# Odd mixer of a decoder step: the pool branch's square-product weights are made one round ahead, in tiles of the attention's pool

## The chip, the cores and the metric

The kernel runs on one core of one Trainium2 chip. The metric is the device time of one execution in microseconds (us), from the first to the last instruction of the program and what lies around it. Less is better.

## The reference, cut to what matters

The reference is one inference step of a two-layer decoder trunk for 512 prompt rows and 32 sample rows (544 in all, width 1024). Each layer is half a SwiGLU block, a mixer, and another half SwiGLU block. The change lies in the mixer of layer 1, the odd mixer:

```python
def odd_mixer(xn, w_in, w_out, c_lin_w, c_scale, ...):
    proj = xn @ w_in                                   # 1024 -> 1024 (pool) + 1536 (q, k, v)
    yc, new_pool = mixer_c(proj[..., :C_WIDTH], pool_state, start_pos, c_lin_w, c_scale)
    q, k, v = d_qkv(proj[..., C_WIDTH:], q_norm, k_norm)
    yd = sliding-window attention of q, k, v (16 heads, window 128, sinks, bias)
    y = jnp.concatenate([yc, yd], axis=-1) @ w_out

def mixer_c(...):                                      # four groups of 256 columns, windows 2, 4, 8, 16
    for gi, win in enumerate(C_WINDOWS):
        pooled = (sum over the last win rows) / count - cur[..., sl]
        outs.append(jnp.einsum('blc,cd->bld', pooled, lin_w[gi]))     # square product, 256 x 256
    y = jnp.concatenate(outs, axis=-1) * scale
```

The two branches, pool (C) and attention (D), need nothing of each other. They meet only in the product with `w_out`.

## The kernel before, in words

Activations lie with the 1024 columns on partitions, eight tiles of 128 by 544. A product in f32 precision is made of three products of halves: each operand is split into a high and a low part (`h`, `l` of an activation; `wh`, `wl`, or `w` for both, of a weight), and `mm` (L208) issues, for each of its k-tiles, high by high, high by low and low by high, in two halves of 272 columns. An accumulator `acc` of `mm` is written by 48 matmuls when the product has eight k-tiles, by 12 when it has two.

`unit` (L185 on) loads up to eight k-tiles of a weight by 256 columns into a staging tile `S` (the pool `stg`, two buffers, DMA issued on SP), and its inner function `part(j)` makes the two halves of 128 columns: ScalarE writes the high part (L193), VectorE the low part (L194). Without `alloc` the halves lie in the pool `wp`, two buffers each; with `alloc` both halves lie in one tile of the pool that `alloc` names. `RR` takes a tile of the pool `rot` (six buffers in the odd mixer), `AA` a tile of the pool `aux` (14 buffers in the odd mixer). `aux` serves the attention: the scores `sc` (two tiles a block), the transposed weights `pT`, the value tiles `vt`, and some fifteen tiles of the sample attention.

`odd` is written in this order: keys and values; four groups `kv` of four heads, each with its query product, query norms (16 small products, L1440, and a chain of twelve small VectorE operations) and four blocks of 128 rows; then the pool branch; then the product with `w_out` for the pool half (`out_proj(w_out, 0, ...)`), and for the attention half.

- A block of the attention is `att_probs` (scores on TensorE, L1514; bias and scale L1518, row maximum L1520 to L1527 on VectorE; four exponentials and one more, L1531 and L1533, on ScalarE; sum, reciprocal and weights, L1534 to L1539, on VectorE) and, one block later in the program, `att_out` (transposes L1553, copies L1555, products with the values L1558, copies L1561). Block 0 of a group is half as wide as the others. `sample_attention` (L1615 on) is made in five steps, interleaved with the last group.
- The pool branch has five rounds, `i` from 0 to 4. In round `i` below 4, `pooled(3 - i)` makes the input product of group `3 - i` (two accumulators of 48 matmuls, weights in `wp`), takes it out of PSUM as `pc` (L1575, L1577), and after the `yield` makes the window sums on GpSimd (`ta`, `tb`, L1599) and the pooled rows `pl` (L1602 on). In round `i` above 0, the square product of group `4 - i` is made: `c_lin_w` is loaded by `unit` with `alloc=RR`, and two accumulators of 12 matmuls follow.

What an engine does is set by the order of its own queue. The program text is not that order: a scheduler takes the instructions in the order of the text as a priority, gives out the buffers of each pool, runs a timeline of its own, and writes one fixed list of instructions for each engine. So instructions of the pool branch can be put between those of the attention, although they stand behind it in the text, wherever their operands and buffers are there in that timeline. An instruction that waits at the head of its engine's list holds back all that stands behind it on that engine.

Of the kernel before, what the change touches and what calls it, by code (L numbers as in the profile page):

```python
# [93 lines left out]
class Trunk:  # L94
# [26 lines left out]
    def TT(self, s, dt=F32):  # L121
        return self.big.tile([P, T], dt, name=self.nm(s), tag="T")
# [29 lines left out]
    @staticmethod  # L152
    def two(ap):
        return ap.rearrange("p (a b) -> p a b", a=2)
# [1174 lines left out]
    def odd(self, nxt):  # L1329
        nc, I, O, two, bc, ch, C = self.nc, self.I, self.O, self.two, self.bc, self.ch, self.C  # L1330
# [3 lines left out]
        sm, RR, TT, AA, ps_ = self.small, self.RR, self.TT, self.AA, self.ps  # L1334
# [35 lines left out]
        for c0, lst, alloc in ((2048, kn, TT), (2304, vf, RR)):  # L1370
            un = self.unit(w_in, 0, 8, c0)
            for j in range(2):
                acc = self.mm(un(j), 8, xs)
# [51 lines left out]
        for kv in range(4):  # L1425
            un = self.unit(w_in, 0, 8, 1024 + kv * 256)
            q2 = []
            for j in range(2):
                acc = self.mm(un(j), 8, xs)
# [35 lines left out]
        yc, pool = [], []  # L1465
        npp = sm("npp", [P, 8, 15])
        nps = sm("nps", [P, 8, 32])

        for i in range(5):
            if i < 4:  # L1470
                stage = self.pooled(3 - i, ext, npp, nps, pool)
                next(stage)
            if i:
                un = self.unit(I["c_lin_w"][0, 4 - i], 0, 2, 0, alloc=RR)
                for j in range(2):
                    m = (4 - i) * 2 + j
                    acc = self.mm(un(j), 2, pool[i - 1])
                    y = TT("yc")
                    with self.tc.high_priority():
                        S.activation(two(y), acc[:, :, :HT], AF.Copy, scale=csc[:, m:m + 1])  # L1480
                    yc.append(y)
            if i < 4:
                next(stage, None)
# [252 lines left out]
    def later(self, odd):  # L1736

        yield from self.columns_gen(("b_norm_g", "c_scale", "a_ln_g", "a_ln_b"), self.TT, self.nc.gpsimd)
        if odd:
            yield from self.bias_pattern()  # L1740
# [80 lines left out]
```

## Time and profile before

| | us |
|---|---|
| median of 3 runs (lowest to highest) | 2270.87 (2264.91 to 2271.98) |
| the profiled execution's own time | 2267.51 |
| its span, first to last instruction | 2265.7 |
| TensorE busy (share of the span) | 2238.1 (99%) |
| VectorE busy | 1708.2 (75%) |
| ScalarE busy | 1063.1 (47%) |
| GpSimd busy | 587.4 (26%) |

The mean granted TensorE clock is 0.994 of full speed. Times in the text are us from the start of the span. In the trace's rows PE is TensorE, PEld its weight load, DVE VectorE, ACT ScalarE, POOL GpSimd, and SPq the DMA queue of SyncE. A row of the timeline has the start, the length, the engine, the line, the operation, what is written and read, the shape, the count of merged instructions, and in brackets the engine's idle time ahead of it with what ended it. Matmuls overlap each other, so their pace is read from start to start.

### The profile page before, as it was taken

What the parts mean: (1) busy time and instruction counts of PE and PEld (TensorE: products, weight loads), DVE (VectorE), ACT (ScalarE), POOL (GpSimd) and SP (SyncE); (2) the same over time, 40 slices, a digit from 0 to 9 for tenths busy, and PEclk for the clock granted to TensorE, in tenths of its full rate; (3) what the DMA queues carried; (4) which work ended last, traced back from release to release, by engine and by line L of the source; (5) the groups of instructions that cost most, each with busy time, mean ns of one, the idle gap of its engine ahead of it and who ended that gap; (6) DMA issues with size and microseconds to landing.
All of it is one profiled execution on the core that took longest, in us unless ns stands there. A gap on an engine that the chain in (4) does not pass through costs nothing.

```text
span 2265.7 us, 42894 instructions
## 1 busy us (share of the span) xinstructions
PE 2238.1 (99%) x17456; PEld 2177.3 (96%) x17456; DVE 1708.2 (75%) x2837; ACT 1063.1 (47%) x1937; POOL 587.4 (26%) x500
## 2 busy tenths in 40 slices
PE   8999999999999999999999999999999999999999
PEld 7999999998889999999999999999988899999998
DVE  7978887675468779888777887876578757888874
ACT  6444444543346354444454444443356544444442
POOL 0434340023330014332403333322033002333320
PEclk9999999999999999999999999999999999999999
DMA  4344443322433233323232332334313223323322
GB/s 149 95 115 99 122 101 114 111 78 76 130 102 96 98 90 103 110 84 110 84 108 63 110 92 89 105 108 142 107 57 114 80 79 107 91 89 106 92 87 68
DMA packets 313862, 224.29 MB, mean 99 GB/s; under 512 B 11640, under 2 KB 306960, under 8 KB 313664
## 3 DMA queue, kind: packets, MB, share of 16 engines
q1 hardware_dynamic: 307800, 206.15, 29.9%
q0 software_dynamic: 5680, 15.34, 2.8%
q8 instruction: 137, 2.24, 0.4%
q14 instruction: 61, 0.50, 0.1%
q10 hardware_dynamic: 184, 0.06, 0.0%
HBM read 203.76 MB, written 17.75 MB: 98 GB/s over the span
## 4 chain that ended last, share of the span: by engine, by line
PE 90%; DVE 4%; ACT 2%; DMA 2%; issue 1%; POOL 1%; SPq 0%; POOLq 0%; DVEq 0%; ACTq 0%
PE acc L208 45%; PE ps L254 34%; PE acc L654 2%; DMA S<-in_ffn_w_gu_dram 1%; PE acc L687 1%; PE ps L974 1%; PE ps L1514 1%; PE ps L1558 1%; POOL S L227 1%; PE ps L1553 1%; DVE wl L237 0%; PE ps L966 0%; POOL S L226 0%; PE ps L368 0%; DVE wl L245 0%
## 5 line engine op out<-in xcount | busy, mean ns | idle before, releaser
L254 PE MATMUL ps<-h,wh 128*128 128x272 f32 x2100 | 602.6, 289 | 5.8 <-ACT g L525 5.8
L254 PE MATMUL ps<-l,wh 128*128 128x272 f32 x2100 | 604.8, 289 | 0.0
L254 PE MATMUL ps<-h,wl 128*128 128x272 f32 x2100 | 602.1, 288 | 0.0
L208 PE MATMUL acc<-h,wh 128*128 128x272 f32 x2768 | 588.7, 292 | 2.0 <-DVE x L694 1.0
L208 PE MATMUL acc<-l,wh 128*128 128x272 f32 x2768 | 585.7, 291 | 0.2 <-DVE l L264 0.2
L208 PE MATMUL acc<-h,wl 128*128 128x272 f32 x2768 | 584.5, 291 | 0.0
L208 PEld LDWEIGHTS acc<-h,wh 128*128 128x128 f32 x2768 | 437.6, 189 | 11.1 <-issue 6.2
L208 PEld LDWEIGHTS acc<-l,wh 128*128 128x128 f32 x2768 | 437.6, 189 | 9.6 <-issue 8.7
L208 PEld LDWEIGHTS acc<-h,wl 128*128 128x128 f32 x2768 | 437.0, 189 | 7.8 <-issue 6.8
L254 PEld LDWEIGHTS ps<-h,wh 128*128 128x128 f32 x2100 | 395.7, 189 | 6.7 <-ACT g L525 6.7
L254 PEld LDWEIGHTS ps<-l,wh 128*128 128x128 f32 x2100 | 396.6, 189 | 0.0
L254 PEld LDWEIGHTS ps<-h,wl 128*128 128x128 f32 x2100 | 396.0, 189 | 0.0
L244 ACT ACTIVATE wh<-S 128x512 fp32r<-128x512 f32 x375 | 235.1, 629 | 322.1 <-PE ps L254 131.7
L245 DVE TENSOR_TENSOR wl<-S,wh 128x512 fp32r<-128x512 f32 x375 | 293.3, 788 | 40.9 <-ACT wh L244 37.9
L228 POOL TENSOR_TENSOR S<-S 128x512 f32<-128x512 f32 x75 | 116.9, 1558 | 509.3 <-DMA S<-in_ffn_w_gu_dram 392.6
L226 POOL TENSOR_TENSOR S<-S 128x512 f32<-128x512 f32 x75 | 102.8, 1371 | 513.3 <-DMA S<-in_ffn_w_gu_dram 235.9
L244 ACT ACTIVATE wh<-D 128x384 fp32r<-128x384 f32 (+1 forms) x224 | 120.7, 540 | 240.9 <-PE ps L254 177.2
L694 DVE SCALAR_TENSOR_TENSOR x<-acc,x 128x544 f32<-128x544 f32 x224 | 160.7, 719 | 65.1 <-PE acc L208 55.4
L245 DVE TENSOR_TENSOR wl<-D,wh 128x384 fp32r<-128x384 f32 (+1 forms) x224 | 176.5, 788 | 9.2 <-ACT wh L244 3.8
L237 DVE TENSOR_TENSOR wl<-S,wh 128x1024 fp32r<-128x1024 f32 x101 | 157.7, 1561 | 12.8 <-ACT wh L236 10.9
L193 ACT ACTIVATE wh<-S 128x1024 fp32r<-128x1024 f32 (+1 forms) x89 | 93.4, 1050 | 156.6 <-PE acc L208 129.8
L236 ACT ACTIVATE wh<-S 128x1024 fp32r<-128x1024 f32 x101 | 106.9, 1059 | 80.8 <-PE ps L254 48.7
(477 smaller groups left out, 2950.6 us busy)
## 6 DMA issues: line engine op xcount, KB each, us to landing
S<-in_ffn_w_gu_dram SPq DMA_DIRECT2D x176, 512.0 KB
D<-in_ffn_w_down_dram SPq DMA_DIRECT2D x96, 384.0 KB
S<-in_ev_w_in_dram SPq DMA_DIRECT2D x18, 1024.0 KB
S<-in_od_w_in_dram SPq DMA_DIRECT2D x10, 1024.0 KB
D<-in_ffn_w_down_dram SPq DMA_DIRECT2D x16, 512.0 KB
S<-in_ev_w_out_dram SPq DMA_DIRECT2D x8, 1024.0 KB
S<-in_od_w_out_dram SPq DMA_DIRECT2D x8, 1024.0 KB
xd<-x POOLq DMA_DIRECT2D x16, 272.0 KB, 2.5
```

Source lines behind the costliest of these rows:

```text
L193: nc.scalar.activation(hi[:, :nk, :n], src, AF.Copy)
L208: self.nc.tensor.matmul(acc[a][:, :HT] if type(acc) is list else acc[:, a, :HT], w[:, k, :], r[:, a * HT:(a + 1) * HT], start=k == order[0 ...
L226: G.tensor_tensor(t["S1"], u0, u1, op=ALU.add)
L227: G.tensor_tensor(t["S2"], t["S1"], g0, op=ALU.subtract)
L228: G.tensor_tensor(t["S3"], g0, u0, op=ALU.subtract)
L236: self.nc.scalar.activation(hi, src, AF.Copy)
L237: self.nc.vector.tensor_tensor(lo, src, hi.bitcast(F32), op=ALU.subtract)
L244: self.nc.scalar.activation(hi, src, AF.Copy)
L245: self.nc.vector.tensor_tensor(lo, src, hi.bitcast(F32), op=ALU.subtract)
L254: self.nc.tensor.matmul(acc, a[:, j, :], r, start=start and j == 0 and q == 0, stop=stop and j == 3 and q == 2, skip_group_check=True)
L654: self.nc.tensor.matmul(acc[a][:, :HT], w[:, k, :], r[:, a * HT:(a + 1) * HT], start=k == 0 and i == 0, stop=k == 7 and i == 2)
L694: nc.vector.scalar_tensor_tensor(two(self.x[m]), acc[:, :, :HT], 0.5, two(self.x[m]), op0=ALU.mult, op1=ALU.add)
```

## The change

In the loop of five rounds, the weights of the square product are now asked for at the head of the round ahead of the one that uses them: in round `i` below 4, ahead of `pooled(3 - i)`, the kernel loads `c_lin_w` of group `3 - i` and makes both halves, `cl = [un(0), un(1)]`. Round `i` above 0 uses the pair that round `i - 1` made. The pair lies in tiles of `aux` (`alloc=AA`), where it lay in tiles of `rot` (`alloc=RR`). The number of loads, of weight halves and of matmuls is the same.

```diff
+        cl = None
         for i in range(5):
+            ws = cl
             if i < 4:
+
+                un = self.unit(I["c_lin_w"][0, 3 - i], 0, 2, 0, alloc=AA)
+                cl = [un(0), un(1)]
                 stage = self.pooled(3 - i, ext, npp, nps, pool)
                 next(stage)
             if i:
-                un = self.unit(I["c_lin_w"][0, 4 - i], 0, 2, 0, alloc=RR)
                 for j in range(2):
                     m = (4 - i) * 2 + j
-                    acc = self.mm(un(j), 2, pool[i - 1])
+                    acc = self.mm(ws[j], 2, pool[i - 1])
```

Lines behind the change move down by four: L1514 of before is L1518 now, L1553 is L1557, L1558 is L1562.

TensorE, second group of heads, from the middle of block 1's `att_out` to block 3's scores. Before, with the pool branch's product of group 2 (`acc_20818`) around the attention's transposes, value products and scores:

```order
L208 MATMUL acc_20818<-l_18584,wh_20814 128x272 x2
L208 MATMUL acc_20818<-h_18583,wl_20815 128x272 x2
L208 MATMUL acc_20818<-h_18618,wh_20814 128x272
L1558 MATMUL ps_19657<-pT_19663,vt_19021 64x256 x2
L1553 MATMUL ps_19667<-cst,sc_19585 128x128 x2
L1553 MATMUL ps_19667<-cst,sc_19592 128x128 x2
L1514 MATMUL ps_19679<-ks_18991,q_19437 128x256
L1514 MATMUL ps_19679<-ks_18991,q_19492 128x256
L1514 MATMUL ps_19686<-kv_18805,q_19437 128x256
L1514 MATMUL ps_19686<-kv_18805,q_19492 128x256
L208 MATMUL acc_20818<-h_18618,wh_20814 128x272
L208 MATMUL acc_20818<-l_18619,wh_20814 128x272 x2
```

The same place now; `acc_20723` is the second accumulator of group 3's product, and these are its last matmuls:

```order
L208 MATMUL acc_20723<-h_18653,wl_20720 128x272 x2
L1557 MATMUL ps_19658<-cst,sc_19585 128x128 x2
L1557 MATMUL ps_19658<-cst,sc_19592 128x128 x2
L1562 MATMUL ps_19657<-pT_19663,vt_19021 64x256 x2
L1557 MATMUL ps_19667<-cst,sc_19585 128x128 x2
L1557 MATMUL ps_19667<-cst,sc_19592 128x128 x2
L1518 MATMUL ps_19679<-ks_18991,q_19437 128x256
L1518 MATMUL ps_19679<-ks_18991,q_19492 128x256
L1518 MATMUL ps_19686<-kv_18805,q_19437 128x256
L1518 MATMUL ps_19686<-kv_18805,q_19492 128x256
L1562 MATMUL ps_19657<-pT_19672,vt_19021 64x256 x2
L1557 MATMUL ps_19710<-cst,sc_19628 128x128 x2
```

From here to the last product of the sample attention (L1729 now) TensorE's list holds no L208 at all; it goes on with group 2 (`acc_20834`) right behind it. In the list of before, 735 matmuls of L208 stand between the same two places: the input products of groups 2, 1 and 0, the four square products and about half of `out_proj` for the pool half.

ScalarE, where the first pair of square-product weights is made. Before, in the second of the four groups of heads, between the exponentials of its blocks 2 and 3:

```order
L1533 ACTIVATE es_19644<-es_19644 128x4
L1555 ACTIVATE pT_19672<-ps_19667 128x512
L193 ACTIVATE wh_21010<-S_21006 128x1024
L193 ACTIVATE w_20934<-S_20932 128x256
L1561 ACTIVATE q_19437<-ps_19657 128x128
```

Now, behind the copies of the last block's transposes (`pT_20599`) and the first copy of the sample attention's output (`sos_20605`):

```order
L1559 ACTIVATE pT_20590<-ps_20585 128x512
L1559 ACTIVATE pT_20599<-ps_20594 128x512
L1726 ACTIVATE sos_20605<-ps_20606 128x256
L193 ACTIVATE w_20650<-S_20648 128x256
L193 ACTIVATE w_20653<-S_20648 128x256
L193 ACTIVATE w_20820<-S_20818 128x256
L193 ACTIVATE w_20823<-S_20818 128x256
L1565 ACTIVATE q_20133<-ps_20584 128x128
L1565 ACTIVATE q_20188<-ps_20584 128x128
L1726 ACTIVATE sos_20605<-ps_20617 128x256
L193 ACTIVATE wh_20830<-S_20826 128x1024
```

The first pair, and the second with it, is made at the end of the attention, and the input weights of group 2 (`wh_20830`) are made behind them.

SP's list, where `S_20648`, `S_20656`, `S_20818` and `S_20826` take the two staging buffers in turn; now:

```order
L171 DMA S_20648<-in_c_lin_w_dram 128x2x256
L171 DMA S_20656<-in_od_w_in_dram 128x8x256
L171 DMA S_20818<-in_c_lin_w_dram 128x2x256
L1667 DMA out_new_k_win_sample_dram<-kc_20333 124x2x256
L1667 DMA out_new_k_win_sample_dram<-kc_20343 124x2x256
L1667 DMA out_new_k_win_sample_dram<-kc_20412 124x2x256
L1667 DMA out_new_k_win_sample_dram<-kc_20422 124x2x256
L171 DMA S_20826<-in_od_w_in_dram 128x8x256
```

Before, the input weights of groups 3 and 2 (`S_20648` and `S_20810` there) were loaded ahead of the first `c_lin_w`; now the load of group 2's input weights (`S_20826`) stands behind the two loads of `c_lin_w` and waits for the staging buffer of the first of them.

## The prediction

> **What bounds the kernel now.** The page first: which engine is full.
>
> ```profile
> span 2265.7 us, 42894 instructions
> PE 2238.1 (99%) x17456; PEld 2177.3 (96%) x17456; DVE 1708.2 (75%) x2837; ACT 1063.1 (47%) x1937; POOL 587.4 (26%) x500
> ```
>
> TensorE is busy in 99% of the span: the kernel is as long as its list of matmuls, and an edit elsewhere gains only where TensorE waits. So the next views are TensorE's waits from 1560 to 1800, around the pool branch, and busy time by stretches there (length, then PE, PEld, DVE, ACT, POOL, granted clock, DMA).
>
> ```profile
> PE acc L208 <- ACT w L193: 1.1, 1, 1.1
> PE acc L208 <- ACT h L263: 0.9, 2, 0.6
> ```
>
> ```profile
> 1690.00:1700.00 10.00, 8.07 (x58) 6.91 (x55) 8.78 (x31) 5.14 (x18) 4.73 (x7) 1.00 0.31 80
> ```
>
> ```profile
> 1679.00:1830.00 151.00, 148.13 (x1103) 129.11 (x1102) 111.19 (x331) 82.72 (x227) 32.41 (x37) 0.97 0.28 92
> ```
>
> ```profile
> 1679.00:1830.00 151.00, 106.77 (x739) 98.31 (x738) 0.97 0.28 92
> ```
>
> The largest wait is the one that the change speaks to: the square product waits 1.1 us for its weights, and 1690 to 1700 has 1.93 us without a matmul. But from 1679 to 1830, where pool branch, attention and half of the first output product run, TensorE stands idle for only 151.0 - 148.1 = 2.9 us. That is all that earlier weights can give back: 0.13%, under the 0.3% (6.8 us) that a measurement of this kernel can tell from no change. The last row is the same stretch with L208 alone: 739 matmuls. They fill TensorE while the attention's chain of small steps runs.
>
> **What the change takes away.** The lists of the changed program, shown above, carry the prediction. With the weight pair in the attention's pool, its tile comes free, in the scheduler's timeline, only when the attention is over. The first pair is made on ScalarE behind the copy of the sample attention's first output, and group 2's input weights stand behind it. TensorE's list has from the middle of the second group of heads to the end of the attention no L208 at all. The work itself is unchanged: as many matmuls, loads and casts as before; but 735 matmuls move from beside the attention to behind it. So the sum has two terms: how long the attention takes by itself (X, from 1679), and the moved matmuls behind it.
>
> The moved matmuls, at their pace in an undisturbed place, and the attention's steps on TensorE:
>
> ```profile
> 1688.44 0.41 PE L208 MATMUL acc<-h,wl 128*128 128x272 f32 x2
> 1688.69 0.41 PE L208 MATMUL acc<-h,wh 128*128 128x272 f32 x2
> ```
>
> ```profile
> 1684.21 0.65 PE L1558 MATMUL ps<-pT,vt 128*64 128x256 f32 x4
> 1684.79 0.66 PE L1553 MATMUL ps<-cst,sc 128*128 128x128 f32 x4
> 1685.38 0.48 PE L1514 MATMUL ps<-ks,q 64*128 64x256 f32 x1
> ...
> 1686.45 0.39 PE L208 MATMUL acc<-h,wh 128*128 128x272 f32 x1
> ```
>
> Two L208 start every 0.25 us, so 739 take 92.4 us. Before, attention and fill together took 151.0; now they take X + 92.4. **The change is X - 58.6 us.** At X = 58.6 nothing is lost. A full block costs TensorE 2 x 0.58 for value products, 2 x 0.59 for transposes and 1.07 for scores, 3.4 us; what matters is how long its chain takes. One block of the second group ran nearly undisturbed:
>
> ```profile
> 1673.46 1.65 DVE L1518 SCALAR_TENSOR_TENSOR sc<-ps,rq,bias 128x256 f32<-128x256 f32 x4
> 1675.03 1.26 DVE L1520 TENSOR_REDUCE mx<-sc 128x2 f32<-128x512 f32 x2
> ...
> 1676.73 0.16 DVE L1527 TENSOR_TENSOR es<-mx,sink 128x4 f32<-128x4 f32 x1
> ...
> 1678.93 0.17 DVE L1534 TENSOR_TENSOR den<-den,es 128x4 f32<-128x4 f32 x1 [1.02 <-ACT es L1533]
> 1679.13 0.18 DVE L1535 RECIPROCAL den<-den 128x4 f32<-128x4 f32 x1
> 1679.35 1.14 DVE L1539 TENSOR_SCALAR sc<-sc,den 128x256 f32<-128x256 f32 x4
> ```
>
> ```profile
> 1676.73 0.51 ACT L1531 ACTIVATE sc<-sc,mx 128x256 f32<-128x256 f32 x1 [2.24 <-DVE mx L1524]
> ...
> 1678.71 0.19 ACT L1533 ACTIVATE es<-es 128x4 f32<-128x4 f32 x1
> ```
>
> VectorE: bias, maximum and three short ones from 1673.46 to 1676.89; then it needs ScalarE's five exponentials, 1676.73 to 1678.90; sum, reciprocal and weights end at 1680.49. That is 7.0 us a block. Blocks overlap little: the new VectorE list has the sum (L1534) of block n ahead of the next block's bias and scale, and waits there for the exponentials, so a block holds VectorE for these 7.0 us. TensorE fits in: from a block's weights to the scores two blocks on it needs transpose, copy, value product, transpose, scores, 0.59 + 0.6 + 0.58 + 0.59 + 1.07 = 3.4 us, while VectorE does the rest of the block between, 7.0 - 1.65 = 5.4. The copy's 0.6 and the other ScalarE steps are in this list:
>
> ```profile
> L1555 ACT ACTIVATE pT<-ps 128x512 f32<-128x512 f32 x20 | 11.8, 589 | 17.9 <-PE ps L1553 17.9
> ```
>
> Block 0 of a group and its query norms, from the fourth group, where the trace has them together:
>
> ```profile
> 1751.80 0.17 DVE L1444 TENSOR_SCALAR qm<-ps 128x16 f32<-128x16 f32 x1 [0.82 <-PE ps L1440]
> ...
> 1755.38 1.13 DVE L1518 SCALAR_TENSOR_TENSOR sc<-ps,rq,bias 128x128 f32<-128x128 f32 x4
> ...
> 1759.79 0.88 DVE L1539 TENSOR_SCALAR sc<-sc,den 128x128 f32<-128x128 f32 x4
> ...
> 1761.35 0.42 DVE L1623 TENSOR_SCALAR sms<-ps 128x256 f32<-128x256 f32 x1
> ```
>
> ```profile
> 1703.31 1.95 PE L1440 MATMUL ps<-cst_odd,qsq 128*128 128x2 f32 x16
> ```
>
> A small block takes 1755.38 to 1760.67, 5.3 us. A group starts when block 2's two halves are through TensorE and ScalarE (3 x 0.6 on either, 3.6), the small products (1.95) and the norm chain (3.6 in the row pair, two unrelated 0.7 in it, so 2.2) are done: 7.8 us behind block 2's weights, of which block 3's remaining 5.4 or less run beside. I take 4.5 for each start, between 2.4 and 7.8.
>
> The terms of X: from 1679 to the weights at 1680.5, less five fill matmuls, 0.9; eight full blocks 8 x 7.0 = 56.0; two small ones 10.6; two starts 9.0. The sample attention's first step ran before from `sms` (L1623, above) to its last small copy:
>
> ```profile
> 1775.74 0.17 DVE L1649 COPY qb<-qs 64x32 f32<-64x32 f32 x1
> ```
>
> Of these 1775.91 - 1761.35 = 14.6 us about half was other work in its way; I take 7.5. For its exponentials, maximum and weights inside the last two blocks I take 5.5, as an estimate, somewhat over one small block. Together 13, between 8 and 18. Then the tail and the restart:
>
> ```profile
> 1817.87 1.97 PE L1719 MATMUL ps<-spT,vc 128*128 128x32 f32 x16
> ```
>
> ```profile
> 1684.61 0.37 SPq L171 DMA_DIRECT2D S<-in_od_w_in_dram  x1
> ```
>
> ```profile
> 1689.88 1.06 ACT L193 ACTIVATE wh<-S 128x1024 fp32r<-128x1024 f32 x1 [0.19 <-DMA S<-in_od_w_in_dram]
> 1690.85 0.40 ACT L193 ACTIVATE w<-S 128x256 fp32r<-128x256 f32 x1
> ```
>
> Tail: last transposes, copies and value products 2.4, sample products 1.9, its copy 0.4, two weight casts on ScalarE 0.8 and one on VectorE 0.4: 6. Only then is the staging buffer free, and the load of group 2's input weights issues; such a load took 1689.88 - 1684.61 = 5.3 us, and its cast 1.06: 6.3. X = 0.9 + 56.0 + 10.6 + 9.0 + 13 + 6 + 6.3 = 101.8, and X - 58.6 = 43.2.
>
> Behind the restart the fill is dense except where its own chain has nothing beside it any more: before the last square product (window sum on GpSimd, pooled rows, split) and between it and the first output product (ScalarE's copies and splits of `yc`). The window sum's row:
>
> ```profile
> 1746.08 2.06 POOL L1599 TENSOR_TENSOR ta<-pc 128x527 f32<-128x527 f32 x1 [3.21 <-DVE nps L1579]
> ```
>
> 2.06 and an estimated 3.3 for taking the group out of PSUM, the pooled rows and the splits, less 24 matmuls (3.0) of the third square product beside it, leave 2.4; the copies and splits of `yc` I take at about as much: 4.5, between 0 and 8.
>
> **The clock.** The granted clock fell in this stretch where small matmuls left the array mostly empty:
>
> ```profile
> 1661.30:1664.70 3.40, 3.40 (x17) 2.70 (x16) 2.92 (x16) 0.43 (x1) 0.00 (x0) 0.50 0.04 14
> 1749.80:1753.20 3.40, 3.40 (x33) 3.25 (x32) 2.05 (x7) 2.91 (x8) 0.00 (x0) 1.00 1.04 374
> 1821.70:1828.50 6.80, 6.80 (x32) 6.80 (x33) 2.38 (x6) 1.84 (x4) 0.00 (x0) 0.50 0.00 1
> ```
>
> ```profile
> 1663.12 1.11 PE L1553 MATMUL ps<-cst,sc 128*128 128x128 f32 x4
> ```
>
> At half clock four transposes take 1.11 instead of 0.66. It fell behind two of these groups of small products and not behind the third (1749.8). Alone, the attention loads TensorE 3.4 of 7.0 us, 49%. At half clock TensorE's 3.4 us between blocks grow to about 6.0, against VectorE's 5.4: 0.6 more a block, 4.8 for eight; 2.3 more at each of two starts; 5.5 in sample and tail: 15 if it lasts all along. The clock at half makes the array look busier, so I expect it to go up and down, and take half, 7.5.
>
> Sum: 43.2 + 4.5 + 7.5 = 55. Against the profiled execution's own 2267.5 (span 2265.7 and 1.8 around it) that is 2322.5. The median of the runs shown lies 3.4 above that execution, so I put the forecast between, at **2324**.
>
> The Trainium skill ("TensorE: Matmul & The Clock Gate", Part 1) says that the array's clock has only two states, half and full, and that a free-running window of about 3.4 us must be busy to raise it; in Part 4 that transposes don't count as busy in the same way. By that rule the half clock would hold nearly all along, and the sum would be 63 instead of 55. The 3.40 and 6.80 us at 0.50 above agree with the first sentence; no run here shows the second.
>
> **The rivals.** Half clock throughout the attention (the rule above as a mechanism of this kernel): nearly half of TensorE's time is idle and much of the rest transposes. For it: the two falls; against it: the third group, and 8.07 busy of 10 without a fall. It gives 43.2 + 4.5 + 15 = 63, 2332.
>
> Blocks overlap more than I have it: VectorE doesn't stand through the exponentials. Then a full block costs 7.0 - 2.2 = 4.9, eight save 17, small blocks and starts about 3: 35, 2304. For it: two blocks are in flight. Against it: the order of VectorE's list.
>
> Not slower: the attention by itself is as quick as TensorE's share of it, X falls under 58.6, and the 2.9 us of waits are gained: 2264.6. Against it, VectorE's attention rows from 1679 to 1830:
>
> ```profile
> L1518 DVE SCALAR_TENSOR_TENSOR sc<-ps,rq,bias 128x256 f32<-128x256 f32 (+1 forms) x40 | 15.9, 448 | 1.4 <-PE ps L1514 1.2
> L1539 DVE TENSOR_SCALAR sc<-sc,den 128x256 f32<-128x256 f32 (+1 forms) x44 | 13.5, 368 | 0.2
> L1520 DVE TENSOR_REDUCE mx<-sc 128x2 f32<-128x512 f32 (+1 forms) x20 | 12.1, 619 | 0.0
> ```
>
> These alone are 41.5 us; 13 for the sample, 12 for tail and restart, and ten waits for exponentials leave no room.
>
> That the change does what it says, a pair ready one round ahead, while the fill stays beside the attention, is ruled out by the lists: their order is fixed.
>
> **How the numbers follow.** Forecast 0.60, half clock throughout 0.22, more overlap 0.15, not slower 0.03. The range takes in both slower rivals, 2304 and 2332, with the bounds of the starts (3.3 more for each of two), of the late gaps (4 less or more) and of the sample (5): 2300 to 2350. Faster by over 0.3% 0.01, within 0.3% 0.02, slower 0.97.
>
> **What would show it.** Right: a stretch of about 100 us from 1680 on with no L208 and TensorE busy 50 to 60%, VectorE waiting in it for ScalarE's exponentials (L1537 now); SP's load of `od_w_in` issued at its end; then some 92 us of dense L208. The pair's wait (1.1 us at L193) gone. Wrong: TensorE near full in that stretch, blocks of under 6 us, or L208 between the blocks.

## The result, and the profile after

| | before | after |
|---|---|---|
| median of 3 runs, us | 2270.87 | 2330.97 (2330.01 to 2331.26) |
| ratio to before, 95% interval | | 1.0277 (1.0260 to 1.0294) |
| the profiled execution's span, us | 2265.7 | 2329.2 |
| mean granted TensorE clock | 0.994 | 0.978 |

The change makes the kernel 60.1 us slower: forecast 2324, with a range of 2300 to 2350. The page first, the span and the busy times of the engines, then from its 40 slices TensorE's busy tenths and its clock:

```profile
span 2329.2 us, 42924 instructions
...
PE 2267.7 (97%) x17456; PEld 2190.4 (94%) x17456; DVE 1712.4 (74%) x2837; ACT 1063.9 (46%) x1937; POOL 587.9 (25%) x500
...
PE   8999999999999999999999999999878899999999
...
PEclk9999999999999999999999999999956999999999
```

The number of matmuls is the same, 17456. Slices 29 to 32, from about 1630 to 1863 (a slice is 58.2 us), aren't full any more, and in two of them, 30 and 31, the clock is down at 0.5 and 0.6. TensorE's "busy" rises by 29.6 us with no new work, since a matmul at half clock counts for longer. So the page alone says where the time is, and that there are two kinds of it: TensorE idle, and TensorE slow.

The timeline of TensorE shows the bare stretch: the last L208 ahead of it and the first behind it, with nothing of L208 between them.

```profile
1675.32 0.41 PE L208 MATMUL acc<-h,wl 128*128 128x272 f32 x2
1791.99 0.82 PE L208 MATMUL acc<-h,wh 128*128 128x272 f32 x2 [0.64 <-ACT wh L193]
```

The same stretch, and the 108 us behind it, by busy time of each engine (columns as before: length, PE, PEld, DVE, ACT, POOL, clock, DMA, GB/s):

```profile
1675.80:1792.00 116.20, 84.56 (x365) 50.33 (x363) 65.68 (x246) 53.02 (x174) 9.35 (x13) 0.60 0.11 32
1792.00:1900.00 108.00, 101.17 (x781) 99.88 (x782) 55.68 (x98) 36.13 (x62) 30.88 (x33) 0.98 0.31 104
```

116.2 us with 365 matmuls, where before 1103 ran in 151.0; no engine is full in it. TensorE shows 84.6 of 116.2, 73%, but at a mean clock of 0.60. Behind it the moved matmuls run nearly without a gap. What TensorE and VectorE wait for in the stretch (us in total, times, longest):

```profile
PE ps L1562 <- ACT pT L1559: 14.6, 18, 2.1
PE ps L1557 <- DVE sc L1543: 11.4, 4, 6.0
...
PE ps L1632 <- DVE qs L1630: 3.0, 1, 3.0
```

```profile
DVE den L1538 <- ACT es L1537: 15.8, 8, 3.3
DVE sc L1522 <- PE ps L1518: 9.2, 5, 3.8
```

They wait for each other in a ring: VectorE for ScalarE's exponentials, TensorE for ScalarE's copies and for VectorE's weights, VectorE for TensorE's scores. Before, L208 stood in each of these waits. The stretch ends as the lists said. ScalarE's and SP's rows:

```profile
1784.00 0.38 ACT L1726 ACTIVATE sos<-ps 128x256 f32<-128x256 f32 x1 [1.87 <-PE ps L1723]
1784.28 1.32 ACT L193 ACTIVATE w<-S 128x256 fp32r<-128x256 f32 x4
1785.78 0.40 SPq L171 DMA_DIRECT2D S<-in_od_w_in_dram  x1
1790.88 2.00 ACT L193 ACTIVATE wh<-S 128x1024 fp32r<-128x1024 f32 x2 [1.66 <-DMA S<-in_od_w_in_dram]
```

The first pair is cast behind the sample attention's first copy; that frees the staging buffer; the load of group 2's input weights issues at 1785.78, is cast from 1790.88 on, and TensorE restarts at 1791.99.

The clock did not do what the forecast says. Half clock was granted in this stretch from 1682.8 to 1703.3, 1710.1 to 1717.0, 1720.4 to 1778.4 and from 1785.2 on: 92 of 116 us. The long one, to 0.2 us:

```profile
1720.60:1778.60 58.00, 44.76 (x176) 25.84 (x173) 30.42 (x126) 26.45 (x87) 1.62 (x2) 0.50 0.09 25
```

In these 58 us TensorE's longest wait is the 3.02 us quoted above (3.0), the others are at most 2.1. TensorE is busy for 77% of them by the profile, and the clock stayed down.

### The profile page after: what moved, and what is told of

It reads as the page before. It is cut to its first block, busy times and chain, and to the rows that moved or that the text cites. A ratio compares the mean times of both kernels' runs of the same rounds, so it can differ in the third digit from the quotient of the medians.

```text
span 2329.2 us, 42924 instructions
## 1 busy us (share of the span) xinstructions
PE 2267.7 (97%) x17456; PEld 2190.4 (94%) x17456; DVE 1712.4 (74%) x2837; ACT 1063.9 (46%) x1937; POOL 587.9 (25%) x500
## 4 chain that ended last, share of the span: by engine, by line
PE 86%; DVE 6%; ACT 3%; DMA 2%; issue 2%; POOL 1%; SPq 0%; DVEq 0%; ACTq 0%; POOLq 0%
PE acc L208 43%; PE ps L254 33%; PE acc L654 2%; DMA S<-in_ffn_w_gu_dram 1%; PE acc L687 1%; ACT sc L1535 1%; PE ps L1518 1%; DVE sc L1522 1%; PE ps L974 1%; DVE wl L237 1%; POOL S L227 1%; PE ps L1562 1%; DVE mx L1524 0%; POOL S L226 0%; PE ps L1440 0%
## 5 line engine op out<-in xcount | busy, mean ns | idle before, releaser
L208 PE MATMUL acc<-h,wh 128*128 128x272 f32 x2768 | 587.8, 291 | 3.9 <-ACT h L263 1.5
L208 PE MATMUL acc<-l,wh 128*128 128x272 f32 x2768 | 583.8, 290 | 0.0
L208 PE MATMUL acc<-h,wl 128*128 128x272 f32 x2768 | 581.8, 290 | 0.0
L208 PEld LDWEIGHTS acc<-h,wh 128*128 128x128 f32 x2768 | 437.5, 189 | 14.3 <-issue 6.0
L208 PEld LDWEIGHTS acc<-l,wh 128*128 128x128 f32 x2768 | 437.8, 189 | 7.3 <-issue 6.5
L208 PEld LDWEIGHTS acc<-h,wl 128*128 128x128 f32 x2768 | 436.3, 189 | 5.2 <-issue 4.2
```

What stands on the lines that cost most here:

```text
L208: self.nc.tensor.matmul(acc[a][:, :HT] if type(acc) is list else acc[:, a, :HT], w[:, k, :], r[:, a * HT:(a + 1) * HT], start=k == order[0 ...
```

## The experiments

**The theory.** The pool in which the pair lies decides. `aux` gives its tiles to the whole attention first; a pair that wants one stands behind the attention, and behind the pair stands the fill. The 60 us are the attention's bare chain. **Rivals:** the early place in the program does it (`c_lin_w` is ahead of the input weights in the two staging buffers); the pool is only a tile or two short; the half clock, not the chain, makes the bare stretch long.

### Place and pool apart: four kernels

With before and after these make a table of two places by three pools. The place is that of after ("early") or of before ("late"); each edit is one word, `alloc=`. The early one in `big`:

```diff
-                un = self.unit(I["c_lin_w"][0, 3 - i], 0, 2, 0, alloc=AA)
+                un = self.unit(I["c_lin_w"][0, 3 - i], 0, 2, 0, alloc=TT)
```

> The kernel after with one word changed: the pair is still made one round ahead, but in tiles of the pool `big` (TT) instead of `aux` (AA). On TensorE's list the pool branch's matmuls stand between the blocks of the attention again (1043 L208 from the first query norms to the end of the sample attention; 1010 before, 275 after). Theory (the lack of a free `aux` tile alone holds the fill back; the early place costs nothing by itself): 2264 to 2273 us, the time of before, and no fall of TensorE's clock that lasts longer than about 10 us in 1680 to 1830. Rival (the early load puts c_lin_w ahead of the input weights in the two staging buffers, and that order alone starves the fill): over 2290 us.

The early one in `rot` has `alloc=RR` at the same line:

> The kernel after with one word changed: the pair is made one round ahead, but in tiles of `rot`, as before. TensorE's list has 1004 L208 in the attention (1010 before, 275 after). Theory (the pool of the pair decides, the early place is free): within 0.3% of before, 2264 to 2276 us. Rival (the early place costs by itself, and the tile of `big` hid that): 2280 us or more.

The late one in `aux`:

```diff
-                un = self.unit(I["c_lin_w"][0, 4 - i], 0, 2, 0, alloc=RR)
+                un = self.unit(I["c_lin_w"][0, 4 - i], 0, 2, 0, alloc=AA)
```

> The kernel before with one word changed: the pair is made where it was, in the round that uses it, but in tiles of `aux`. TensorE's list has 394 L208 in the attention (275 after, 1010 before): 119 more than after, and the first pair still stands behind the attention. Theory (the tile pool decides, the place only how far the fill gets before it stalls): 119 x 0.125 = 15 us less than after, 3 to 6 more of it if the clock is held up for as long, so 2310 to 2318 us. Rival (the early place is the cause): 2264 to 2275 us.

And the late one in `big`, `alloc=TT` at that line:

> The kernel before with one word changed: the pair is made in the round that uses it, in tiles of `big` instead of `rot`. 912 L208 in the attention, 98 fewer than before. By the slope that two runs gave (60 us for the 735 matmuls that left the attention, some 9 for 119, so 0.08 us for each), 98 fewer cost 8 us: 2275 to 2280 us. Rival (the matmuls that left lie where the attention has other cover, since the fill never stops for long): same as before, 2264 to 2274.

Measured, as a ratio to before with its 95% interval, and L208 in the attention by TensorE's list:

| pool | late | early |
|---|---|---|
| `rot` | 1 (before), 1010 | 1.0047 (1.0030 to 1.0063), 1004 |
| `big` | 1.0078 (1.0053 to 1.0103), 912 | 1.0007 (0.9994 to 1.0020), 1043 |
| `aux` | 1.0234 (1.0209 to 1.0259), 394 | 1.0277 (1.0260 to 1.0294), 275 |

The early place alone, with tiles of `big`, costs nothing; tiles of `aux` alone, at the old place, cost 2.3%. So the pool is the cause, and the rival of the place falls. The bare stretch of the late kernel in `aux` begins a block later:

```profile
1692.50:1794.40 101.90, 77.73 (x335) 46.96 (x335) 59.58 (x222) 48.83 (x159) 10.51 (x12) 0.60 0.09 26
```

Two expectations missed. 119 more L208 inside the attention gave back 0.43% (9.8 us, each ratio uncertain by some 0.2%), not 15: the time that they need is partly paid there, since the blocks that they stand in get longer. And `rot` early and `big` late are measurably slower than before although nearly all of their fill is in place; the price by count (8 us for 98) is half of the 17.7 measured for `big` late. In that kernel's trace TensorE waits 5.9 us for the high halves of weights between 1640 and 1850, where before waited 1.1, and once 3.8 us for a copy with nothing to fill it:

```profile
PE acc L208 <- ACT w L193: 5.9, 2, 3.7
PE ps L1558 <- ACT pT L1555: 3.8, 1, 3.8
```

In the trace of `rot` early TensorE waits 4.3 us for accumulators that VectorE is still taking out (L1583) and once 2.9 us for a copy (L1559). These waits are a part of the two prices; the rest stays open.

### The staging buffer

After, with `c_lin_w` loaded into a tile of its own:

```diff
-    def unit(self, w, k0, nk, c0, ncol=256, alloc=None):
+    def unit(self, w, k0, nk, c0, ncol=256, alloc=None, own=None):
...
-        s = self.stage(w, k0, nk, c0, ncol)
+        if own:
+            s = own("S")[:, :nk * ncol].rearrange("p (k m) -> p k m", k=nk)
+            nc.sync.dma_start(s, w[k0 * P:(k0 + nk) * P, c0:c0 + ncol].rearrange("(k p) m -> p k m", p=P))
+        else:
+            s = self.stage(w, k0, nk, c0, ncol)
...
-                un = self.unit(I["c_lin_w"][0, 3 - i], 0, 2, 0, alloc=AA)
+                un = self.unit(I["c_lin_w"][0, 3 - i], 0, 2, 0, alloc=AA, own=TT)
```

> The kernel after, but each c_lin_w is loaded into a tile of `big` of its own instead of one of the two staging buffers, so that a pair that waits for an `aux` tile no longer holds a staging buffer which the input weights of the next group need. TensorE's list has 394 L208 in the attention (275 after). Theory (the wait for the `aux` tile holds the list of ScalarE's weight halves too, the staging buffer only adds to it): 15 to 20 us less than after, 2310 to 2318 us. Rival (the staging buffer is the whole of it): near before, under 2280 us. If the fill that is gained only moves: same as after, 2328 to 2333.

Measured 1.0238 (1.0214 to 1.0261), with 394 L208 in the attention: 0.39% (9 us) less than after, where 15 to 20 were expected. So the held staging buffer is the smaller part: it keeps 119 L208 out of the attention. The tile that the pair waits for is the larger part. It is the number of the late kernel in `aux`, whose list has the same 394.

### How short the pool is

One tile more:

```diff
-    POOLS = {"even": MIX(4, 18, 3, 5), "odd": MIX(6, 14, 4, 5)}
+    POOLS = {"even": MIX(4, 18, 3, 5), "odd": MIX(6, 15, 4, 5)}
```

> The kernel after with 15 tiles in `aux` instead of 14 (no more fit into memory). Theory (the pair stands behind the whole attention in the order in which the pool gives out its tiles, so one tile more moves it by at most one tile's life): the list still has 275 L208 in the attention, 2327 to 2335 us. Rival (the pool is one tile short): near before, under 2290.

And the sample attention's tiles taken out of `aux`:

```diff
-        sm, RR, TT, ps_ = self.small, self.AA, self.TT, self.ps
+        sm, RR, TT, ps_ = self.small, self.TT, self.TT, self.ps
```

> The kernel after with the sample attention's tiles moved from `aux` to `big`, so that fewer tiles of `aux` are given out between the attention's last block and the pair. TensorE's list has the same 275 L208 in the attention. Theory (the pair stands behind the tiles of the whole attention in the pool's order): the time of after, 2326 to 2335 us. Rival (the sample attention holds the tiles that the pair needs): under 2310.

With the sample's tiles elsewhere the ratio is 1.0279 (1.0248 to 1.0310), that of after: they don't hold the pair back. With 15 tiles it is **slower still**, 1.0388 (1.0361 to 1.0414), where the theory said no change. Both lists have 275 L208 in the attention, and the casts of all eight `c_lin_w` halves stand behind its last block. But with 15 tiles the same 275 stand earlier: 267 of them ahead of the second group's query norms, where after has 199, so that 8 are left for the second group and not 76, and the fill is used up two blocks sooner. Its bare stretch:

```profile
1683.20:1815.40 132.20, 93.16 (x401) 55.73 (x400) 73.67 (x274) 59.59 (x199) 9.35 (x13) 0.63 0.10 28
```

132.2 us against 116.2, 12 blocks' reciprocals in it against 10. From the first group's query norms to this stretch it takes 53.3 us where after takes 56.1, for as many L208 and two blocks fewer, and TensorE has no idle time from 1640 to 1683 (43.00 us busy of 43.00). So two more blocks without fill cost 16.0 us and save 2.8 ahead of the stretch: what counts is how many blocks are left without any L208, and not only the number of L208. A block that gets more of them than its waits can take runs at TensorE's pace, and they are then missing in a later one.

That is some 13 of the 24 us by which this kernel is slower than after. Another 10 lie ahead of the attention: the first query norms start at 1629.66, after's at 1619.39, with 5965 L208 started ahead of them in both. TensorE waits there, from 1560 on, for two things that cost after 0.2 us together, and the clock falls twice:

```profile
PE acc L208 <- DVE kv L1376: 3.8, 1, 3.8
PE ps L1362 <- DMA pst<-in_state_pool_dram: 3.3, 2, 2.6
```

How the 15th tile brings these waits about stays open. The rival (a pool that is one tile short) falls, and so does my count of 0.08 us for each matmul.

### What the half clock costs: four kernels

Three are after with products added that nothing reads (128 by 256 in f32, into an unused half of a PSUM tile), in each block from block 1 of the second group of heads on; the fourth is after itself once more. The texts on record say that the rest of TensorE's order in the attention is that of after. The traces show that it is not, nor are the lists of VectorE and ScalarE; this is taken up below. In the first kernel, six products stand behind each block's last value products:

```diff
+        if (kv, blk) >= (1, 1):
+            for r in range(6):
+                PE.matmul(po[:, 256:512], pT[:, r % 4 * P:r % 4 * P + P], self.xs[r][0][:, 0:256].bitcast(F32),
+                          start=True, stop=True)
```

> The kernel after with six extra products in each block from block 1 of the second group of heads on (128 by 256 in f32, into a half of a PSUM tile that nothing reads; nothing of the output changes). The order of the rest of TensorE's list in the attention is that of after. They tell what the half clock costs there: after shows half clock for some 92 of the 116 us without L208. If the clock follows how busy TensorE is, it stays full for most of the stretch, and the attention is shorter by up to 10 us: 2319 to 2328 us. If the half clock is not what makes the stretch long (VectorE's and ScalarE's chain is), the extra products lie in TensorE's idle time and the time is 2329 to 2333. If they stand in the way of the chain: up to 2345, and then the clock is up and the blocks are longer all the same.

Measured 1.0346 (1.0322 to 1.0370), 2347.5 us, just above the last of the three ranges. The half clock in 1670 to 1840 falls from 96 to 51 us, and the bare stretch grows all the same, from 116 to 133 us: the products stand in the way, and what the clock gave is not seen.

Next, in the wait between a block's first transposes and the copy that they feed (`r` up to 4, then up to 3):

```diff
+            if hf == 0 and (kv, blk) >= (1, 1):
+                for r in range(4):
+                    PE.matmul(po[:, 256:512], self.xs[r][0][:, 0:128].bitcast(F32), self.xs[r][0][:, 0:256].bitcast(F32),
+                              start=True, stop=True)
             pT = self.AA("pT")
             S.activation(pT[:, :512], pst, AF.Copy)
```

> The kernel after with four extra products (128 by 256 in f32, into a half of a PSUM tile that nothing reads) in each block from block 1 of the second group of heads on, placed behind the first four transposes, where TensorE waits some 0.7 to 2 us for ScalarE's copy; nothing of the output changes, and the rest of TensorE's order is that of after. At full clock they are 11 x 4 x 0.24 = 10.4 us, most of it inside waits. If the half clock costs the attention its 15 us and a busier TensorE lifts it: 2320 to 2329. If the clock stays down, they take 0.4 us each there: 2331 to 2341. If the clock rises and the time does not fall, the half clock is not what the stretch is long by.

> As the kernel with four extra products in each block's first wait, but with three: at full clock 0.71 us, as much as the 0.69 us that TensorE waits there for ScalarE's copy, so that they stand in nobody's way while the clock is up. The measure is the time from the last L208 ahead of the attention's bare stretch to ScalarE's first copy of the sample attention's output: 1675.8 to 1784.0, 108.2 us, after the change, and 108.1 with four extra products, where the clock was at half for 48 us instead of 92. If the half clock costs the attention 15 us and the four products hid that gain, it is now 98 to 103 us, and the time 2320 to 2326. If the half clock costs little, since the chain over VectorE and ScalarE sets the pace: 105 to 109 us, 2324 to 2332.

The price of a product in both texts is wrong by a factor of two. Each product in f32 stands in the trace as two matmuls: the 33 of the second kernel are the 66 of this row (its columns: shortest, median and longest in ns, first and last start).

```profile
L1560 PE MATMUL ps<-h x66: 379/382/793, 1676.2 to 1772.4; 128*128 128x256 f32 x66
```

At full clock twelve such matmuls take 2.86 us (in the kernel with six products), six 1.46 and eight 1.89, so three products take 1.5 us and four 1.9; both are longer than the 0.69 us wait that they were meant for. Measured: four 1.0269 (1.0246 to 1.0291), the time of after; three 1.0238 (1.0216 to 1.0261), 2320.0 us. Since the second is only 0.4% under after, and the executions of after and of the kernel with the sample's tiles in `big` differed by 3.4 us in the stretch, it was measured again beside after:

> The kernel with three extra products in each block's first wait once more, beside the kernel after on the same chip, to tell a difference of a few tenths of a per cent: the first measurement gave 1.0238 times the time of before, after and the kernel with the sample's tiles in `big`, which has its list, 1.0277 and 1.0279; but the stretch up to the sample's first copy differed between those two by 3.4 us (108.3 and 104.9) with one list. If the half clock has a price of some 15 us for 92 us of it, this is again 6 to 10 us quicker than the kernel after. If the first result was the spread between executions: within 3 us of it.

> The kernel after, unchanged, on the same chip as the kernel with three extra products in each block. Both theories: 1.025 to 1.030 times the time of before, 2323 to 2334 us, and half clock for 80 to 95 us of the stretch.

2324.13 us and 1.0248 (1.0234 to 1.0263) against 2330.64 us and 1.0278 (1.0263 to 1.0292): 6.5 us quicker, with 33 products more. The stretch in the two, first after:

```profile
1677.50:1792.40 114.90, 84.32 (x364) 50.18 (x362) 64.37 (x242) 53.02 (x174) 9.35 (x13) 0.60 0.11 32
```

```profile
1676.20:1784.40 108.20, 80.58 (x431) 54.74 (x429) 65.96 (x250) 53.01 (x174) 9.32 (x13) 0.83 0.12 35
```

431 matmuls for 364, and yet less TensorE time (80.6 us for 84.3), since the clock is 0.83 and not 0.60. From the last to the first L208, both executions of each kernel: 116.7 and 115.3 us with 92 us of half clock in each, 108.3 and 108.6 with 40.5 and 36.6. So the stretch is some 7.6 us shorter with 53 us less of half clock. Up to the sample's first copy on ScalarE it is 100 us in both executions, as was expected for a costly half clock. But the clock is not all that differs. VectorE's reciprocals, one for each block, from the fourth group's first block on, with the sample attention's first copy out of PSUM (`sms`); first after, then with three extra products:

```profile
1735.96 0.18 DVE L1539 RECIPROCAL den<-den 128x4 f32<-128x4 f32 x1
...
1738.58 0.42 DVE L1627 TENSOR_SCALAR sms<-ps 128x256 f32<-128x256 f32 x1 [1.53 <-PE ps L1625]
...
1756.83 0.18 DVE L1539 RECIPROCAL den<-den 128x4 f32<-128x4 f32 x1
...
1770.90 0.17 DVE L1539 RECIPROCAL den<-den 128x4 f32<-128x4 f32 x1
...
1777.08 0.17 DVE L1539 RECIPROCAL den<-den 128x4 f32<-128x4 f32 x1
```

```profile
1733.94 0.42 DVE L1631 TENSOR_SCALAR sms<-ps 128x256 f32<-128x256 f32 x1 [0.95 <-PE ps L1629]
...
1734.79 0.18 DVE L1539 RECIPROCAL den<-den 128x4 f32<-128x4 f32 x1
...
1752.35 0.18 DVE L1539 RECIPROCAL den<-den 128x4 f32<-128x4 f32 x1
...
1762.57 0.18 DVE L1539 RECIPROCAL den<-den 128x4 f32<-128x4 f32 x1
...
1765.30 0.18 DVE L1539 RECIPROCAL den<-den 128x4 f32<-128x4 f32 x1
```

`sms` stands behind the first reciprocal in after's list and ahead of it in the other, and the last two blocks are 2.7 us apart instead of 6.2. The scheduler wrote other lists for the kernel with extra products, so its 6.5 us hold the order and the clock together.

The kernel with the sample's tiles in `big` tells the two apart in two places. Its list too has `sms` ahead of the first reciprocal, so it is not quite after's; the granted clock there is at half nearly throughout. Its first step of the sample attention, from that reciprocal to the next, takes 18.8 us (1734.44 to 1753.23). After takes 20.9, and the two executions with three extra products take 19.0 and 17.6. So much of what the first step gained came with the order. From the second reciprocal to the third, after and this kernel have the same instructions in the same order on TensorE, ScalarE and VectorE (two matmuls and two copies fall on the border), and what differs in the traces is the clock; first after:

```profile
1756.83:1770.90 14.07, 12.47 (x48) 6.62 (x48) 7.55 (x25) 6.34 (x27) 0.00 (x0) 0.50 0.01 1
```

```profile
1753.23:1764.05 10.82, 6.46 (x46) 3.92 (x48) 7.52 (x26) 6.07 (x25) 0.00 (x0) 0.94 0.01 2
```

Here, where the sample's small products and a block's stand on TensorE one behind the other, half clock costs 3.2 us. In the third group of after it costs a block next to nothing:

```profile
1703.70 0.18 DVE L1539 RECIPROCAL den<-den 128x4 f32<-128x4 f32 x1
...
1710.36 0.18 DVE L1539 RECIPROCAL den<-den 128x4 f32<-128x4 f32 x1
...
1717.16 0.18 DVE L1539 RECIPROCAL den<-den 128x4 f32<-128x4 f32 x1
```

The first of these two blocks ran at full clock and the second at half: 6.7 and 6.8 us. With the query norms' products at two starts (3.58 us at half clock, 1.95 at full), half clock is worth some 6.5 us in the places that these rows show. What all 92 us of it cost is not shown.

Four products lift the clock as far as three (44 us of half) and end at 116.1 us; their 22 matmuls more take 5.2 us at full clock. The rival that the half clock alone makes the stretch long falls: at 0.83 it still lasts 108 us, and before L208 filled it.

The Trainium skill ("TensorE: Matmul & The Clock Gate", Part 1) gives the clock two states and judges it by free-running windows of about 3.4 us. The traces agree: every half-clock stretch quoted is a multiple of 3.4 us (6.8, 20.5, 58.0), and only 0.5 and 1.0 occur. In its section "Why this matters for your kernels" the Trainium skill's same title asks, against drops of the clock, for no idle gap of TensorE over about 3 us. The falls at 1682.8 and 1710.1 lie in waits of 6.0 and 3.3 us and agree; the one at 1720.4 came with no wait above 0.7 us in the nine us ahead of it, so here that isn't enough. What the Trainium skill says of transposes (Part 4 of that title) was not tried by itself.

## Why the prediction was right, point by point

**What bounds it, and what the change takes away** were right. The order of TensorE's list told the place, the length in work and the cause of the restart; the signs named beforehand are there: a bare stretch (116 us, not 100), VectorE's wait for L1537, the load of `od_w_in` at its end, and the dense L208 behind it. One is off: TensorE is busy for 73% of the stretch, not 50 to 60, since its matmuls take longer at half clock. The wait for the pair (1.1 us) is gone and weighs nothing.

**The size.** The sum was 55 us, the measured difference of the spans 63.5 (of the medians 60.1). The profiled execution of after reaches the stretch 4.85 us earlier than that of before: the same transposes stand at 1680.43 before and 1675.58 after. So the stretch costs 68.4, and that the median came within 7 us of the forecast is in part luck: the sum is 13 short, and 4.85 came back ahead of the stretch. 2.0 of these are there at the second group's query norms (1657.27 after, 1659.29 before), with 6164 L208 started in both; whether they are the change's is not shown. Term by term, X from the point that was 1679 before and is 1674.15 here (a block runs from VectorE's weights, L1543, to the next block's; a start from the last weights to the next group's first bias, L1522; the tail ends where SP issues the load):

| term of X | predicted, full clock | measured |
|---|---|---|
| up to the last L208 | 0.9 | 1.5 |
| second group's last two blocks | 14.0 | 14.7 |
| start of the third group | 4.5 | 9.2 |
| its four blocks | 26.3 | 26.0 |
| start of the fourth group | 4.5 | 6.3 |
| its small block | 5.3 | 5.2 |
| sample, first step | 7.5 | 11.4 |
| last three blocks, with the sample | 26.5 | 29.9 |
| tail | 6.0 | 7.4 |
| restart | 6.3 | 6.2 |
| X | 101.8, and 7.5 for the clock | 117.8 |

The block, from one undisturbed block of before, was right to 0.3 us in the third group's 26, the restart to 0.1. In the second group's last two blocks the 14.7 hide two errors that offset each other. The prediction had VectorE take block n's sum ahead of the next block's bias; here block 3's bias comes first, so the blocks overlap. And VectorE's short operations, 0.17 us elsewhere, take up to 1.43 while GpSimd makes window sums (1679.67 to 1686.80; that these are the cause is not shown):

```profile
1681.06 0.86 DVE L1522 SCALAR_TENSOR_TENSOR sc<-ps,rq,bias 128x256 f32<-128x256 f32 x2
...
1684.05 1.02 DVE L1538 TENSOR_TENSOR den<-den,es 128x4 f32<-128x4 f32 x1
...
1685.19 1.43 DVE L1528 TENSOR_SCALAR mx<-mx 128x4 f32<-128x4 f32 x1
```

X is 16.0 above 101.8, and the clock was given 7.5 of them. What was mis-sized:

- *"I expect it to go up and down, and take half, 7.5"* (the clock). It stayed down for 92 of 116 us. Some 6.5 us of its cost show in rows; the whole is open, and with it whether the 15 of the working for half clock all along were right. The rival "half clock throughout" with 2332 was nearer to the 2331 measured than the forecast. The argument against it, one group of small products without a fall, was read from a place with L208 on either side. The split was off: not 0.6 a block, but 0.1 (6.7 and 6.8 us), and 3.2 in one place beside the sample attention.
- *"I take 4.5 for each start"*. 9.2 and 6.3. At the third group's start nothing ran beside anything: TensorE's and VectorE's rows are a single chain from the last transposes to the first scores' bias.

```profile
1690.41 1.12 PE L1557 MATMUL ps<-cst,sc 128*128 128x128 f32 x4
1692.28 1.12 PE L1562 MATMUL ps<-pT,vt 128*64 128x256 f32 x4 [0.75 <-ACT pT L1559]
1693.33 3.58 PE L1440 MATMUL ps<-cst_odd,qsq 128*128 128x2 f32 x16
```

```profile
1696.94 0.17 DVE L1444 TENSOR_SCALAR qm<-ps 128x16 f32<-128x16 f32 x1 [2.38 <-PE ps L1440]
...
1699.25 0.17 DVE L275 SCALAR_TENSOR_TENSOR rq<-rs_t,rs_r 128x16 f32<-128x16 f32 x1
1699.52 0.61 DVE L1522 SCALAR_TENSOR_TENSOR sc<-ps,rq,bias 128x128 f32<-128x128 f32 x2
```

  The query norms' products stand behind block 3's last value products on TensorE's list, so block 3 isn't passed beside the start; and at half clock they take 3.58 us, not 1.95. That is above even the bound of 7.8.
- The sample, 13 with bounds of 8 to 18: 11.4 and 8.9 (29.9 less three blocks of 7.0), 20.3, beyond the upper bound. 3.2 of it are the clock's by the rows above. ScalarE's two loads of a function table lie in it too; before had both, but the second, ahead of the exponentials, stands in none of the rows from which the 13 was made:

```profile
1737.89 1.28 ACT L1628 ACT_TABLE_LOAD   x1
...
1753.13 1.28 ACT L1535 ACT_TABLE_LOAD   x1 [0.44 <-DVE mx L1528]
```

- Behind the restart, 4.5 for late gaps: 63.5 + 4.85 - 59.2 (X - 58.6) = 9.2 are to be explained. 6.8 of the 108 us are idle (108.0 - 101.2), and the first 3.5 us of the fill ran at half clock, which is another 1.7. One wait among the idle ones was not foreseen, twice for the PSUM accumulators of a group that is still being taken out:

```profile
PE acc L208 <- DVE nps L1583: 3.9, 2, 2.0
PE acc L208 <- ACT h L263: 2.5, 2, 1.5
```

  In the attention, its small products stood between the groups; with the groups back to back nothing does.

**The other rivals** fell by the same table: blocks at 7 us leave no room for "more overlap", and X is twice the 58.6 at which nothing would be lost.

## What to carry to other kernels

A buffer's pool is a place in a queue: a small early operand that takes its tile from a pool which a long stage uses comes only when that stage is done, and all that needs it, and all that shares its staging buffer, comes with it. Read the new list of the bounding engine for what no longer stands between the waits of a chain, and price the bare chain from one undisturbed round of it. What fill a stage keeps is judged by how many of its rounds have any, not by its number of instructions, and small products left alone may have to be priced at half clock. An extra product put in as a probe changes the engines' lists as well: compare the lists before the difference is given to one cause.

## What was not expected of the hardware

- Work added into waits made the program quicker: 66 more matmuls, 6.5 us less. The granted clock of the stretch rose from 0.60 to 0.83, and the engines' lists changed with it, so the 6.5 us are not the clock's alone.
- The same instructions in the same order took 14.07 us at half clock and 10.82 us at 0.94 where small products stand one behind the other, while a plain block took 6.8 at half and 6.7 at full.
- The clock can stay down without a long wait: 58 us at half clock with TensorE shown busy in 44.8 of them, and no wait longer than 3.02 us.
- A product of 128 by 256 in f32 runs as two matmuls, 0.24 us each at full clock (twelve in 2.86 us).
